# A row softmax on one core: six head loads of 16 rows per partition become three of 32

## The chip, the core and the metric

The kernel runs on one core of one Trainium2 chip. The time is device microseconds of one execution, the median of several. A core has the compute engines TensorE (PE, not used here), VectorE (DVE), ScalarE (ACT) and GpSimd (POOL); SyncE (SP) computes nothing and only issues transfers here. The transfers are carried out by the core's 16 DMA engines. On-chip memory has 128 partitions.

## The reference

The input is `x`, 16 x 1024 x 512 in float32: 16384 rows of 512 numbers, 33.55 MB. The output has the same shape. Each row is replaced by its softmax:

```python
x_max = np.max(x, axis=-1, keepdims=True)
exp_x = np.exp(x - x_max)
return (exp_x / np.sum(exp_x, axis=-1, keepdims=True)).astype(np.float32)
```

## The kernel before

The 16384 rows are spread over 128 partitions, 128 rows to each. "Row" below means one of these 128 rows per partition; row 5 is thus 128 rows of `x`, one in each partition, and takes 2 KiB of a partition.

**Groups.** Compute works on 16 groups of 8 rows. For each group there are four steps. DVE takes the negated row maxima (`rowmax`, line 164, an M in the order below). ACT runs eight activations, one per row, that write exp(x - max) over x and accumulate the row sums (line 195). DVE takes the reciprocals of the eight sums (line 170), and then either POOL (P in the order) or DVE (V) multiplies the group by them in place (line 172). The string `VECTOR` at line 44 is the order of DVE's instructions, written out by hand: `M5` is the maxima of group 5, `P4` the reciprocals of group 4 with the multiply on POOL, `V12` the reciprocals of group 12 with the multiply on DVE. DVE executes them in this order, and a step that has to wait holds up all that follow it there.

**Transfers.** All loads and stores are issued by SP on a single queue, in the order of the list `ORDER` (line 22): eight loads L and eight stores S, each of 16 rows, that is 32 KiB in each partition and 4 MiB in all. The first `AHEAD` entries (6) are loads issued at once at the start (line 126); the first of them is moved ahead of the program's opening barrier (`AT_HEAD`, line 49). Of the others, a store (line 152) waits on SP for the multiplies of the groups that it holds (`scaled`), and a load waits for the store whose place it takes (`stored`). SP waits in order: what stands behind a waiting entry of `ORDER` is not issued.

**The buffer.** `held` has room for 96 rows (`RING`). Loads (96,112) and (112,128) go to the places of rows 0 to 31 and so wait for stores (0,16) and (16,32). The numbers in brackets are the first row and the row after the last.

**Where rows lie in DRAM.** `in_dram` (line 87) takes the entry of `BLOCKS` that holds the rows and gives each partition a contiguous stretch of it: with a block of 16 rows, partition p has rows 16p to 16p + 15 of the block's 2048, so 32 KiB in one piece, and the next partition's piece follows at once. Loads and stores use the same mapping, so the output is independent of it.

**Semaphores.** Each load has its own semaphore (`loaded`), which the first `rowmax` that meets its rows waits for; `maxed`, `expd`, `to_pool` and `to_vector` pass groups from engine to engine.

Of the kernel before, what the change touches and what calls it, by code (L numbers as in the profile page):

```python
# [1 line left out]

# [4 lines left out]

F32 = mybir.dt.float32
EXP = mybir.ActivationFunctionType.Exp
AX = mybir.AxisListType.X  # L10

GROUP = 8
GROUPS = 16
RING = 12 * GROUP

BLOCKS = [(0, 16), (16, 32), (32, 48), (48, 64), (64, 80), (80, 96), (96, 112), (112, 128)]
ORDER = [
    ("L", (0, 16)),
    ("L", (16, 32)),
    ("L", (32, 48)),
    ("L", (48, 64)),
    ("L", (64, 80)),
    ("L", (80, 96)),
    ("S", (0, 16)),
    ("S", (16, 32)),  # L30
    ("S", (32, 48)),
    ("L", (96, 112)),
    ("L", (112, 128)),
    ("S", (48, 64)),
    ("S", (64, 80)),
    ("S", (80, 96)),
    ("S", (96, 112)),
    ("S", (112, 128)),
]
AHEAD = 6  # L40

VECTOR = """
    M0 M1 P0 M2 P1 M3 P2 M4 P3 M5 P4 M6 P5 M7 P6 M8 P7 M9 P8 M10 P9 M11
    P10 M12 P11 M13 V12 M14 V13 M15 V14 V15
"""

AT_HEAD = {mybir.EngineType.SP: 1}

def loads_at_the_head(nc):

    main, body = nc.main_func.blocks[0], nc.main_func.blocks[1]
    for engine, count in AT_HEAD.items():
        loads = [
            i
            for i in body.instructions
            if i.engine == engine and type(i).__name__ == "InstDMACopy"  # L60
        ][:count]
        barrier = next(
            n
            for n, i in enumerate(main.instructions)
            if i.engine == engine and type(i).__name__ == "InstDrain"
        )
        for load in loads:
            body.instructions.remove(load)
        main.instructions[barrier:barrier] = loads


@with_exitstack
def kernel(
    ctx: ExitStack,
    tc: tile.TileContext,
    x: bass.AP,
    out: bass.AP,
):
    nc = tc.nc
    nc.at_finalize(loads_at_the_head)  # L80
    P = nc.NUM_PARTITIONS

    d = x.shape[-1]
    x_rows, out_rows = x.flatten_outer_dims(), out.flatten_outer_dims()
    assert x_rows.shape[0] == GROUPS * GROUP * P

    def in_dram(rows, a, b):

        first, last = next(k for k in BLOCKS if k[0] <= a and b <= k[1])
        block = rows[first * P : last * P].rearrange("(p r) d -> p r d", p=P)  # L90
        return block[:, a - first : b - first, :]

    held = nc.alloc_sbuf_tensor("held", [P, RING, d], F32).ap()
    shift = nc.alloc_sbuf_tensor("shift", [P, GROUPS * GROUP], F32).ap()
    sums = nc.alloc_sbuf_tensor("sums", [P, GROUPS * GROUP], F32).ap()
    recip = nc.alloc_sbuf_tensor("recip", [P, GROUPS * GROUP], F32).ap()

    loads = [k for what, k in ORDER if what == "L"]
    stores = [k for what, k in ORDER if what == "S"]
    loaded = {k: nc.alloc_semaphore(f"loaded{k[0]}") for k in loads}  # L100
    scaled = [nc.alloc_semaphore(f"scaled{g}") for g in range(GROUPS)]
    stored = {k: nc.alloc_semaphore(f"stored{k[0]}") for k in stores}
    maxed = nc.alloc_semaphore("maxed")
    expd = nc.alloc_semaphore("expd")
    to_pool = nc.alloc_semaphore("to_pool")
    to_vector = nc.alloc_semaphore("to_vector")

    def take(engine, semaphore, n):

        engine.wait_ge(semaphore, n).then_inc(semaphore, -n)  # L110

    def rows(a, b):
        assert a // RING == (b - 1) // RING
        return held[:, a % RING : (b - 1) % RING + 1, :]

    def meets(k, a, b):
        return k[0] < b and a < k[1]

    def group(g):
        return g * GROUP, (g + 1) * GROUP  # L120

    def stats(t, g):
        return t[:, g * GROUP : (g + 1) * GROUP]

    def load(k):
        copy = nc.sync.dma_start(out=rows(*k), in_=in_dram(x_rows, *k))
        copy.then_inc(loaded[k], 16)
        return copy

    with tc.manual_schedule():
        for _, k in ORDER[:AHEAD]:
            tc.no_tile_sem_insts.add(load(k).ins.name)
    tc.close()
    tc.compile()  # L137

    taken, done = set(), set()
    for what, k in ORDER[AHEAD:]:  # L140
        if what == "L":
            for s in stores:
                if meets(s, k[0] - RING, k[1] - RING) and s not in taken:
                    take(nc.sync, stored[s], 16)
                    taken.add(s)
            load(k)
        else:
            for g in range(GROUPS):
                if meets(k, *group(g)) and g not in done:
                    take(nc.sync, scaled[g], 1)  # L150
                    done.add(g)
            nc.sync.dma_start(out=in_dram(out_rows, *k), in_=rows(*k)).then_inc(
                stored[k], 16
            )


    seen = set()

    def rowmax(g):
        for k in loads:  # L160
            if meets(k, *group(g)) and k not in seen:
                take(nc.vector, loaded[k], 16)
                seen.add(k)
        nc.vector.reduce_max(  # L164
            out=stats(shift, g), in_=rows(*group(g)), axis=AX, negate=True
        ).then_inc(maxed, 1)

    def scale(g, engine, ready):
        take(nc.vector, expd, 1)
        nc.vector.reciprocal(out=stats(recip, g), in_=stats(sums, g)).then_inc(ready, 1)  # L170
        take(engine, ready, 1)
        engine.tensor_mul(  # L172
            out=rows(*group(g)),
            in0=rows(*group(g)),
            in1=stats(recip, g).unsqueeze(2).to_broadcast([P, GROUP, d]),
        ).then_inc(scaled[g], 1)

    for step in VECTOR.split():
        what, g = step[0], int(step[1:])
        if what == "M":  # L180
            rowmax(g)
        elif what == "V":
            scale(g, nc.vector, to_vector)
        else:
            scale(g, nc.gpsimd, to_pool)


    nc.scalar.preload_act_table(EXP)  # L188

    with nc.scalar.Fori(0, GROUPS) as i:  # L190
        take(nc.scalar, maxed, 1)
        for r in range(GROUP):
            row = held[:, bass.ds(i % (RING // GROUP) * GROUP + r, 1), :]
            at = bass.ds(i * GROUP + r, 1)
            act = nc.scalar.activation(  # L195
                out=row,
                in_=row,
                func=EXP,
                bias=shift[:, at],
                scale=1.0,  # L200
                accum_out=sums[:, at],
            )
        act.then_inc(expd, 1)


    for k in stores:
        if k not in taken:
            take(nc.sync, stored[k], 16)


# [1 line left out]
_INS = ['x']  # L212
_OUTS = [((16, 1024, 512), 'float32')]


# [23 lines left out]
```

## Time and profile before

| | |
|---|---|
| median of 3 runs | 160.15 us (160.12 to 160.21) |
| the profiled execution | 160.14 us, with a span of 158.8 us |
| DVE busy | 90.6 us (57%) |
| ACT busy | 92.0 us (58%) |
| POOL busy | 84.0 us (53%) |
| DMA queue's packets | 98.9% of 16 engines' span |
| bytes moved | 33.55 MB read, 33.55 MB written, 423 GB/s |

The span runs from the first recorded instruction to the last event; the profiled execution's own time is 1.34 us longer. A figure such as x16 counts instructions. In the timelines a row gives its start in the span, the time to its end, the engine, the line of the kernel, the operation and the tiles, and in square brackets the idle time before it with what ended it; "held<-in_x_dram" is a load into `held`, "out_dram<-held" a store. A row of DMA issues gives the KB of each and the median time from issue to landing, the latter being when the completion has been seen. A row with x11 merges eleven instructions that follow each other. In a view by windows the columns are the stretch, its length, the busy time of DVE, ACT and POOL with their counts, the granted TensorE clock, the share of the DMA engines' time, and GB/s; a packet is booked in the stretch in which it starts, so shares can pass 1.

### The profile page before, as it was taken

What the parts mean: (1) busy time and instruction counts of PE and PEld (TensorE: products, weight loads), DVE (VectorE), ACT (ScalarE), POOL (GpSimd) and SP (SyncE); (2) the same over time, 40 slices, a digit from 0 to 9 for tenths busy, and PEclk for the clock granted to TensorE, in tenths of its full rate; (3) what the DMA queues carried; (4) which work ended last, traced back from release to release, by engine and by line L of the source; (5) the groups of instructions that cost most, each with busy time, mean ns of one, the idle gap of its engine ahead of it and who ended that gap; (6) DMA issues with size and microseconds to landing.
All of it is one profiled execution on the core that took longest, in us unless ns stands there. A gap on an engine that the chain in (4) does not pass through costs nothing. (4 is left out here: it accounts for less than half of the span.)

```text
span 158.8 us, 747 instructions
## 1 busy us (share of the span) xinstructions
DVE 90.6 (57%) x36; ACT 92.0 (58%) x257; POOL 84.0 (53%) x16
## 2 busy tenths in 40 slices
DVE  0008959777977977887700000795999998640000
ACT  0300699999999999999993000059934929200000
POOL 0000009999999999999999999259200000000000
DMA  7999999999999998999999999999999999999996
GB/s 264 470 454 396 413 487 421 396 454 470 396 396 487 437 396 380 413 396 454 470 396 421 462 437 396 446 479 396 421 446 454 396 437 473 413 404 454 446 413 264
DMA packets 2305, 67.12 MB, mean 423 GB/s; under 512 B 256, under 2 KB 256, under 8 KB 256
## 3 DMA queue, kind: packets, MB, share of 16 engines
q1 hardware_dynamic: 2304, 67.11, 98.9%
q14 instruction: 1, 0.01, 0.0%
HBM read 33.55 MB, written 33.55 MB: 423 GB/s over the span
## 5 line engine op out<-in xcount | busy, mean ns | idle before, releaser
L195 ACT ACTIVATE held<-held,shift x128 | 90.3, 712 | 40.0 <-ACTq L110 40.0
L172 POOL TENSOR_TENSOR held<-held,recip 128x4096 f32<-128x4096 f32 x12 | 83.8, 7015 | 28.0 <-POOLq L110 28.0
L164 DVE TENSOR_REDUCE shift<-held 128x8 f32<-128x4096 f32 x16 | 70.3, 4399 | 33.2 <-DVEq L110 33.2
L195 ACT ACTIVATION_READ_ACCUMULATOR held<-held,shift x128 | 24.6, 192 | 0.0
L172 DVE TENSOR_TENSOR held<-held,recip 128x4096 f32<-128x4096 f32 x4 | 18.3, 4570 | 0.6
L170 DVE RECIPROCAL recip<-sums 128x8 f32<-128x8 f32 x16 | 3.2, 201 | 16.5 <-DVEq L110 16.5
L188 ACT ACT_TABLE_LOAD x1 | 1.3, 1283 | 3.9 <-PEq L137 3.9
L223 POOL MEMSET const-float32-0.0<- 128x1 f32 x1 | 0.1, 98 | 0.2 <-issue 0.2
L223 POOL MEMSET const-uint8-127<- 128x1 uint8 x1 | 0.1, 102 | 0.0
L223 POOL MEMSET const-bfloat16-1.0<- 128x1 bf16 x1 | 0.1, 101 | 0.0
L223 POOL MEMSET const-float32-1.0<- 128x1 f32 x1 | 0.1, 98 | 0.0
## 6 DMA issues: line engine op xcount, KB each, us to landing
held<-in_x_dram SPq DMA_DIRECT2D x8, 4096.0 KB, 29.7
out_dram<-held SPq DMA_DIRECT2D x8, 4096.0 KB, 28.3
```

The costliest lines, as they stand in the source:

```text
L164: nc.vector.reduce_max(out=stats(shift, g), in_=rows(*group(g)), axis=AX, negate=True).then_inc(maxed, 1)
L170: nc.vector.reciprocal(out=stats(recip, g), in_=stats(sums, g)).then_inc(ready, 1)
L172: engine.tensor_mul(out=rows(*group(g)), in0=rows(*group(g)), in1=stats(recip, g).unsqueeze(2).to_broadcast([P, GROUP, d]),).then_inc(scal ...
L188: nc.scalar.preload_act_table(EXP)
L195: act = nc.scalar.activation(out=row, in_=row, func=EXP, bias=shift[:, at], scale=1.0, accum_out=sums[:, at],)
L223: nc = _bacc.Bacc("TRN2", target_bir_lowering=False, num_devices=1)
```

## The change

The six loads of rows 0 to 95 become three, of 32 rows each: 64 KiB in each partition, 8 MiB in all. `BLOCKS` follows them: the first 96 rows are laid out in DRAM in blocks of 32 rows, so that a load's 64 KiB of a partition are one contiguous piece. The stores of these rows stay at 16 rows, and each now takes half of every partition's 64 KiB. The last two loads, the last two stores and their blocks are as before. `AHEAD` is 3 in place of 6: the same rows are loaded at the start. In DVE's order, groups 12 and 13 are multiplied on POOL in place of DVE. With the blocks, row r of a partition holds another row of `x` than before, which changes no instruction.

```diff
-BLOCKS = [(0, 16), (16, 32), (32, 48), (48, 64), (64, 80), (80, 96), (96, 112), (112, 128)]
+BLOCKS = [(0, 32), (32, 64), (64, 96), (96, 112), (112, 128)]
 ORDER = [
-    ("L", (0, 16)),
-    ("L", (16, 32)),
-    ("L", (32, 48)),
-    ("L", (48, 64)),
-    ("L", (64, 80)),
-    ("L", (80, 96)),
+    ("L", (0, 32)),
+    ("L", (32, 64)),
+    ("L", (64, 96)),
     ("S", (0, 16)),
     ("S", (16, 32)),
     ("S", (32, 48)),
     ("L", (96, 112)),
     ("L", (112, 128)),
     ("S", (48, 64)),
     ("S", (64, 80)),
     ("S", (80, 96)),
     ("S", (96, 112)),
     ("S", (112, 128)),
 ]
-AHEAD = 6
+AHEAD = 3

 VECTOR = """
     M0 M1 P0 M2 P1 M3 P2 M4 P3 M5 P4 M6 P5 M7 P6 M8 P7 M9 P8 M10 P9 M11
-    P10 M12 P11 M13 V12 M14 V13 M15 V14 V15
+    P10 M12 P11 M13 P12 M14 P13 M15 V14 V15
 """
```

## The prediction

> **What bounds the kernel now.** I read the page's slices and queue table first, then the windows by stage, then the queue's own issues with their times to landing, last the engines' timelines. The first view says which resource is never idle:
>
> ```profile
> span 158.8 us, 747 instructions
> DVE 90.6 (57%) x36; ACT 92.0 (58%) x257; POOL 84.0 (53%) x16
> DMA  7999999999999998999999999999999999999996
> GB/s 264 470 454 396 413 487 421 396 454 470 396 396 487 437 396 380 413 396 454 470 396 421 462 437 396 446 479 396 421 446 454 396 437 473 413 404 454 446 413 264
> DMA packets 2305, 67.12 MB, mean 423 GB/s; under 512 B 256, under 2 KB 256, under 8 KB 256
> q1 hardware_dynamic: 2304, 67.11, 98.9%
> ```
>
> Three compute engines are each under 60% busy; the 16 DMA engines are full from the second slice to the last but one. 2304 packets are 16 transfers of 128 large packets (one partition's 32 KiB each) and of 16 small ones (the 256 "under 512 B"). The chain of waits shows only 3% of the span, because it does not follow the DMA queue; it is of no use here. Next, the rate by stage (columns: stretch, its length, DVE, ACT and POOL busy, clock, DMA share, GB/s):
>
> ```profile
> 42.00:52.00 10.00, 7.76 (x5) 10.00 (x29) 10.00 (x3) 1.00 0.99 429
> 52.00:57.00 5.00, 3.85 (x3) 5.00 (x15) 5.00 (x1) 1.00 0.97 419
> 57.00:62.00 5.00, 4.41 (x2) 5.00 (x15) 5.00 (x2) 1.00 0.98 347
> 62.00:72.00 10.00, 8.36 (x4) 10.00 (x29) 10.00 (x2) 1.00 1.04 449
> ```
>
> Bytes are booked when a packet starts, so 419 to 449 is one steady rate. 347 GB/s at 57 to 62 us, with the DMA engines as busy as ever, is a real dip: packets take longer there. It lies where the loads end and the first store begins. The issues put numbers on it (median us from issue to landing; the six loads in issue order):
>
> ```profile
> 1.17 0.42 SPq L126 DMA_DIRECT2D held<-in_x_dram  x1
> held<-in_x_dram SPq DMA_DIRECT2D x1, 4096.0 KB, 30.4
> ...
> 1.65 0.47 SPq L126 DMA_DIRECT2D held<-in_x_dram  x1
> held<-in_x_dram SPq DMA_DIRECT2D x1, 4096.0 KB, 39.7
> ...
> 65.44 0.33 SPq L152 DMA_DIRECT2D out_dram<-held  x1
> out_dram<-held SPq DMA_DIRECT2D x1, 4096.0 KB, 25.4
> ...
> 140.91 0.33 SPq L152 DMA_DIRECT2D out_dram<-held  x1
> out_dram<-held SPq DMA_DIRECT2D x1, 4096.0 KB, 17.9
> ```
>
> Issue plus time to landing gives the landings. Loads: the first at 12.2, the second at 0.79 + 21.0 = 21.8 (the median of the first two is 16.6, midway from 12.2), the third at 1.17 + 30.4 = 31.6, the fourth at 41.4, the fifth at 2.16 + 48.9 = 51.05 and the sixth near 61.5 by the medians of neighbouring pairs. Stores (0,16), (16,32), (32,48): 71.1, 80.9, 90.8. Loads (96,112), (112,128): 100.3, 110.1. The last five stores: 119.9, 129.6, 139.4, 149.1, 158.8. So 4 MiB lands every 9.7 us, in order of issue, and the span ends with the sixteenth. Two places cost more: the first landing takes 12.2 us, 2.5 us over the pitch, and the sixth load is 10.5 us behind the fifth, a stall of 0.8 us. The turn from load (112,128) to store (48,64) at 110 us shows none.
>
> Last, how far compute is ahead of this queue:
>
> ```profile
> 12.33 8.75 DVE L164 TENSOR_REDUCE shift<-held 128x8 f32<-128x4096 f32 x2 [12.33 <-DVEq L110]
> 23.46 76.76 POOL L172 TENSOR_TENSOR held<-held,recip 128x4096 f32<-128x4096 f32 x11 [23.02 <-POOLq L110]
> 105.16 7.01 POOL L172 TENSOR_TENSOR held<-held,recip 128x4096 f32<-128x4096 f32 x1 [4.94 <-POOLq L110]
> ```
>
> Store (32,48) is issued at 65.4 and its turn comes at 80.9, when the store before it lands. A transfer issued before its turn costs the end nothing.
>
> **The change, part by part.**
>
> *Fewer, longer packets.* Six loads of 128 x 32 KiB become three of 128 x 64 KiB. Bytes are the same. Each DMA engine gets 24 large packets in place of 48, and 3 fewer small ones. No packet of 64 KiB is in the trace, so I bound it. Fixed part of a packet: in a 0.4 us window the one 8 KiB instruction packet has 4.8% of 16 engines, 0.307 us; from 22 to 52 us, 400 large packets have 101.2% of 30 us x 16, 1.214 us each. Four times 0.307 is 1.228, so (1.228 - 1.214) / 3 = 5 ns is fixed per packet (1 to 9 ns with the rounding of 4.8%). 24 packets fewer save 0.12 us (0.02 to 0.2). The small packets: 8 x 1.214 = 9.71 us is already the pitch, so three of them are at most 0.03 us. The other end: the pitch between like neighbours varies from 9.69 to 9.78 us; should the long packets sit at its upper end, six times 0.05 is a loss of 0.3. I take -0.15, because the steady rows are the nearest, and keep -0.25 and +0.3.
>
> The Trainium skill, page "DMA: Bandwidth & Descriptors", section "Bandwidth", gives one transfer about 2.0 us fixed plus bytes at 436 GB/s, and advises large transfers. By that, three transfers fewer would save 6 us, an estimate from the page. The trace disagrees for a queue that is never empty: 9.7 us per 4 MiB is 432 GB/s with the fixed part in it.
>
> *Three SP issues less.* Six take 3.13 us at the start, three some 1.6. They lie beside the first load, and the first one stays at 0. Nothing.
>
> *The first data come later.* Row maxima 0 wait for 8 MiB: the second load's landing now, 21.8 in place of 12.2. DVE, ACT and POOL all start 9.6 us later. What it meets, with POOL's 76.76 / 11 = 6.98 us per group: P0 starts at 33.1, so store (0,16) is issued at 37.5 + 9.6 = 47.1 (turn at 61.5), (16,32) at 61.1 (turn 71.1), (32,48) at 75.0 (turn 80.9). The last has least room, 5.9 us. SP then issues load (96,112), which stands behind it on SP, at about 75.4 where it was 71.28; its turn is at 90.8. Load (112,128) still waits for store (16,32), landed at 80.9. Store (48,64) follows P7 at 89 (turn 110.1), (64,80) P9 at 103 (119.9), (80,96) P11 at 117 (129.6). Row maxima 4 and 8, which now wait for loads landing near 41.2 and 61.3, come at 44 and 67. ACT's 12 groups end near 94.4, still before load (96,112) lands. All hidden; cover gone means one us per us beyond these margins.
>
> *Groups 12 and 13 go from DVE to POOL.* DVE loses two of its 4.43 to 5.00 us multiplies, POOL gains two of 7.01. POOL: P11 ends at 117, P12 at 124, P13 at 131; store (96,112) is issued at 131 (125.6 before; turn 139.4, 8 us of room). On DVE, M14 no longer stands behind V12 (started 111.45), nor M15 behind V13, so V15 ends near 133 in place of 140.8; store (112,128) follows at 133 (turn 149.1). Neither bounds. Nothing.
>
> *The stores keep 32 KiB per partition*, but in the first 96 rows their pieces, and the loads' rows, now lie 64 KiB apart in DRAM instead of 32. No row shows another pitch; see the rivals. I take nothing. The 0.8 us stall I keep: the first store still follows an unbroken run of loads.
>
> **Sum.** The profiled execution took 160.14 (span 158.8 and 1.34 around it), against a median of 160.15. 158.8 - 0.15 + 1.34 = 160.0 us. Range of this case alone: 159.85 to 160.45.
>
> **The rivals.**
>
> *The stall goes* (faster): it comes once, after 48 large packets in a row, and not at 110 us after 16. If the long run of queued packets causes it, 24 of them may not. Against it: what is special may simply be the first store, which stays. 160.0 - 0.8 = 159.2.
>
> *The stall grows* (slower): only packets in flight at the turn at 57 to 62 us are stretched, 0.8 us on 32 KiB ones. If it scales with the packet, the last 64 KiB packets lose 1.6: 160.8. It is slower by my bound from a stall of 1.3 us on.
>
> *The pitch in DRAM* (slower): 12 of the 16 transfers, 116 us, now run with rows 64 KiB apart. One per cent of rate lost there is 1.2 us: 161.2; it decides from 0.4%. Nothing in the trace shows sensitivity: loads and stores, in all regions, keep 9.7 us. The Trainium skill, same page, section "Latency and other measured facts", has copies slowing at large power-of-two row pitches, from 207 GB/s each way at 512 KiB to 164 at 2 MiB; by that 64 KiB is still harmless. No run here shows it.
>
> *The queue runs dry* (slower): it needs store (32,48) after 80.9, that is compute 15.5 us late instead of 9.6. Were POOL a whole group (6.98 us) further behind, 9.6 + 7.0 - 15.5 = 1.1 us: 161.1.
>
> *A fixed cost per transfer* (faster): if the first landing's 2.5 us over the pitch were paid by every load, three fewer give 160.14 - 7.5 = 152.6. The 9.7 us pitch speaks against it. The skill's formula above would give 154.1.
>
> *The row is cut in two again* by the queue, and packets stay 32 KiB: 160.14.
>
> **How the numbers follow.** Plain small gain 0.67 (160.0); cut rows 0.05 (160.14); stall gone 0.11; stall grown 0.09; pitch 0.05; dry queue 0.02; fixed cost 0.01. A change below 0.2% (0.32 us) is about what a measurement of this kernel cannot tell from none. Faster 0.11 + 0.01 = 0.12, same 0.72, slower 0.16. The range takes in both stall cases with 0.1 us to spare, 159.1 to 160.9; pitch, dry queue and fixed cost, 0.08, stay outside.
>
> **What would show it.** Right: 1872 packets on the queue (13 x 16 small, 384 of 64 KiB, 1280 of 32 KiB; 2256 if the rows are cut), DMA full from slice 2 to 39, landings of loads near 21.8, 41.2 and 61.4, then every 9.7 us; POOL starting at 33; SP never issuing a store after its turn. Wrong: a landing pitch other than 9.7 in the first 96 rows, a different dip near 57 to 62 us, or a slice of DMA below 9 in the middle.

## The result: 0.2% slower, where 0.1% faster was forecast

The changed kernel takes 160.49 us (median of 13 runs, 160.36 to 161.26) against 160.12 for the kernel before in the same comparison: a ratio of 1.0022, with a 95% interval of 1.0012 to 1.0032. The forecast was 160.0, with 159.1 to 160.9 as its range and 0.16 for "slower". The time lies in the range; the sign is wrong. It lies 0.04 us above the range that I gave this case alone, 159.85 to 160.45. The wide range holds it only because it had room for a longer stall, and I had given that another reason.

The page of the changed kernel, the lines that answer to those shown of before:

```profile
span 159.2 us, 741 instructions
DVE 88.0 (55%) x34; ACT 91.8 (58%) x257; POOL 102.1 (64%) x18
DMA  7996996997989989999999999999999999999994
DMA packets 1873, 67.12 MB, mean 422 GB/s; under 512 B 208, under 2 KB 208, under 8 KB 208
q1 hardware_dynamic: 1872, 67.11, 98.6%
```

1872 packets: a row of 64 KiB in one partition does move whole. The queue still never runs empty. By the trace's packet records a 64 KiB packet takes 2.418 us and a 32 KiB packet 1.213. (A digit below 9 in the first slices of DMA comes from long packets being booked where they start.)

The same stretches as before in the view by windows, of the changed kernel:

```profile
52.00:57.00 5.00, 3.84 (x3) 5.00 (x15) 5.00 (x2) 1.00 0.97 419
57.00:62.00 5.00, 3.85 (x3) 5.00 (x15) 5.00 (x2) 1.00 1.02 354
62.00:72.00 10.00, 7.99 (x3) 10.00 (x31) 10.00 (x2) 1.00 1.03 446
72.00:82.00 10.00, 8.61 (x4) 10.00 (x30) 10.00 (x3) 1.00 0.99 426
82.00:92.00 10.00, 5.06 (x4) 10.00 (x29) 10.00 (x3) 1.00 0.97 419
```

and the last stretch of the kernel before:

```profile
82.00:92.00 10.00, 0.00 (x0) 2.91 (x9) 10.00 (x2) 1.00 0.97 419
```

The dip at the turn from loads to stores is still there. What differs is beside store (32,48), from 82 to 92 us: ACT is busy for all of it where it was busy for 2.9 us, because compute runs 9.7 us later.

Where do the 0.35 us of the span come from? The issue of load (112,128), which SP makes when store (16,32) has landed, and its time to landing; first before, then after:

```profile
80.96 0.34 SPq L126 DMA_DIRECT2D held<-in_x_dram  x1
held<-in_x_dram SPq DMA_DIRECT2D x1, 4096.0 KB, 29.1
```

```profile
81.06 0.34 SPq L123 DMA_DIRECT2D held<-in_x_dram  x1
held<-in_x_dram SPq DMA_DIRECT2D x1, 4096.0 KB, 29.3
```

Up to 81 us 0.10 us are lost; by the landing at 110.06 and 110.36, 0.30. So 0.2 us go in between, while the transfers are the same as before.

A transfer has landed when the last of the 16 DMA engines is done with it, and each engine works through its own share of every transfer, 8 of the 128 large packets. The packet records do not name the engine; a packet is put down to the engine whose packet before it ended as this one started. The small packets that end each engine's share show the spread. After 158.2 us there are, before and then after, in 158.2:158.5 and 158.5:158.9:

```profile
DMA packets 2, 0.00 MB, mean 0 GB/s; under 512 B 2, under 2 KB 2, under 8 KB 2
DMA packets 0, 0.00 MB, mean 0 GB/s; under 512 B 0, under 2 KB 0, under 8 KB 0
```

```profile
DMA packets 1, 0.00 MB, mean 0 GB/s; under 512 B 1, under 2 KB 1, under 8 KB 1
DMA packets 1, 0.00 MB, mean 0 GB/s; under 512 B 1, under 2 KB 1, under 8 KB 1
```

The last engine ends at 158.31 us before; after, one ends at 158.34 and the last at 158.65. By the packet records, from the first packet's start to the first engine's end is 156.42 us before and 156.38 after, and to the mean of the 16 ends 156.80 in both: the engines as a whole are no slower. From the first engine's end to the last one's is 0.87 before and 1.25 after. In both kernels this last engine is one whose packets, from 66 us on, often take 14 to 50 ns (once 130) more than 1.213, several one after the other, while the others' hardly ever do. (In the kernel before, two engines start a packet in the same nanosecond at 135.25 us. I follow the one whose packets go on being long; if they are the other way round, the slowed engine ends at 158.24 and not last.)

### The profile page after: what moved, and what is told of

It reads as the page before. It is cut to its first block, busy times and chain, and to the rows that moved or that the text cites. A ratio compares the mean times of both kernels' runs of the same rounds, so it can differ in the third digit from the quotient of the medians.

```text
span 159.2 us, 741 instructions
## 1 busy us (share of the span) xinstructions
DVE 88.0 (55%) x34; ACT 91.8 (58%) x257; POOL 102.1 (64%) x18
## 3 DMA queue, kind: packets, MB, share of 16 engines
q1 hardware_dynamic: 1872, 67.11, 98.6%
## 5 line engine op out<-in xcount | busy, mean ns | idle before, releaser
L169 POOL TENSOR_TENSOR held<-held,recip 128x4096 f32<-128x4096 f32 x14 | 101.9, 7315 | 32.7 <-POOLq L107 32.7
L192 ACT ACTIVATION_READ_ACCUMULATOR held<-held,shift x128 | 25.1, 196 | 0.0
L169 DVE TENSOR_TENSOR held<-held,recip 128x4096 f32<-128x4096 f32 x2 | 15.7, 7857 | 0.3
```

Source lines behind the costliest of these rows:

```text
L169: engine.tensor_mul(out=rows(*group(g)), in0=rows(*group(g)), in1=stats(recip, g).unsqueeze(2).to_broadcast([P, GROUP, d]),).then_inc(scal ...
L192: act = nc.scalar.activation(out=row, in_=row, func=EXP, bias=shift[:, at], scale=1.0, accum_out=sums[:, at],)
```

## The experiments

Two numbers are read from each trace's packet records. *Long packets beside stores* is the time that packets take above their plain 1.213 or 2.418 us (0.611 for the 16 KiB packets of early8_fine), summed over all engines, from 66 to 81 us (stores (0,16) and (16,32)) and from 81 to 91 us (store (32,48)). *The turn* is the same sum from 56 to 61 us, divided by 16: what an engine loses there. Times are medians; the ratio is to the kernel before on the same chip. The ratio is not the plain quotient of the two medians, and differs from it by up to 0.0009, or 0.15 us.

| kernel | us (before) | ratio, 95% interval | long packets, 66-81 / 81-91, ns | turn, us |
|---|---|---|---|---|
| before | 160.12 | | 296 / 47 | 0.88 |
| changed | 160.49 (160.12) | 1.0022 (1.0012 to 1.0032) | 279 / 277 | 1.01 |
| swap_only | 160.14 (160.20) | 0.9994 (0.9981 to 1.0008) | 302 / 51 | 0.81 |
| loads_only | 160.48 (160.20) | 1.0012 (0.9998 to 1.0027) | 293 / 293 | 1.06 |
| late_only | 160.34 (160.20) | 1.0010 (0.9995 to 1.0024) | 280 / 248 | 0.71 |
| layout_only | 160.39 (160.20) | 1.0009 (0.9995 to 1.0023) | 295 / 84 | 1.03 |
| early_big | 160.57 (160.20) | 1.0021 (1.0012 to 1.0030) | 312 / 208 | 0.96 |
| early8 | 160.04 (160.20) | 0.9992 (0.9983 to 1.0000) | 282 / 102 | 0.61 |
| act_only | 160.00, one run | | 181 / 42 | 0.63 |
| no_act | 166.48, one run | | 0 / 0 | 0.74 |
| copy16 | 159.80 (160.20) | 0.9966 (0.9954 to 0.9979) | 0 / 61 | 0.65 |
| copy32 | 160.09 (160.20) | 0.9991 (0.9982 to 1.0001) | 0 / 0 | 1.07 |
| loads32_old | 160.31 (160.20) | 1.0005 (0.9995 to 1.0016) | 284 / 310 | 0.85 |
| turn_early | 160.32 (160.20) | 1.0005 (0.9996 to 1.0014) | see below | see below |
| copy_load64 | 160.04 (160.21) | 0.9989 (0.9980 to 0.9998) | 0 / 0 | 1.04 |
| copy_store64 | 159.77 (160.21) | 0.9977 (0.9968 to 0.9985) | 0 / 0 | 0.85 |
| act_no_sum | 159.95, one run | | 40 / 74 | 0.72 |
| early8_fine | 160.16 (160.25) | 0.9995 (0.9981 to 1.0008) | 295 / 116 | 0.67 |
| early8_again | 160.12 (160.25) | 0.9992 (0.9983 to 1.0002) | 296 / 175 | 0.52 |

The 61 of copy16 lies at the end of its stretch, where store (32,48) gives way to a load. Other kernels have long packets there too while ACT rests: copy_load64 one of 219 ns at 92.5 us, act_only one of 87 at 92.2, early8 80 in all from 88 to 91. So the second column is not ACT's alone. In the changed kernel 132 of its 277 ns are one packet at 89.1 us. From 81 to 88 us, clear of that place, the sums are 21 before and 136 in the changed kernel, 116 in late_only, 126 in loads_only and loads32_old, 98 in early_big, 19 in layout_only and early8.

**The parts of the change, one at a time.** Four theories: late compute, the swap to POOL, the layout in DRAM, the long packets.

```diff
 swap_only, to the kernel before:
-    P10 M12 P11 M13 V12 M14 V13 M15 V14 V15
+    P10 M12 P11 M13 P12 M14 P13 M15 V14 V15
```

> The kernel before with groups 12 and 13 multiplied on POOL (P12, P13 for V12, V13) and nothing else. Layout and packet theories, and late compute: no change, within 0.1 us of the kernel before. Theory of the swap (POOL and DVE hold each other up at the end, V15 took 10.6 us in the changed kernel): 0.3 us slower, most of the 0.37 us that the changed kernel lost.

```diff
 loads_only, to the changed kernel:
-    P10 M12 P11 M13 P12 M14 P13 M15 V14 V15
+    P10 M12 P11 M13 V12 M14 V13 M15 V14 V15
```

> The changed kernel with V12, V13 kept: three loads of 32 rows, compute 9.6 us late, no swap. Theory of the swap: 0.05 to 0.15 us faster than the kernel before. The three others (late compute, layout, long packets): 0.25 to 0.4 us slower, as the changed kernel.

```diff
 late_only, to the kernel before, in rowmax:
-            if meets(k, *group(g)) and k not in seen:
+            if meets(k, *(group(g) if g else (0, 32))) and k not in seen:
```

> The kernel before, all transfers as they were, but the first row maxima wait for load (16,32) too, so compute runs 9.6 us later. Theory of late compute (more work of ACT and DVE lies beside the stores, one DMA engine of the 16 is slowed by it, and the slowest ends the kernel): 0.2 to 0.4 us slower, and the skew between the first and the last DMA engine's end grows from 0.87 us toward 1.2. Layout and packets: within 0.1 us, skew unchanged.

```diff
 layout_only, to the kernel before:
-BLOCKS = [(0, 16), (16, 32), (32, 48), (48, 64), (64, 80), (80, 96), (96, 112), (112, 128)]
+BLOCKS = [(0, 32), (32, 64), (64, 96), (96, 112), (112, 128)]
```

> The kernel before with the DRAM blocks of the changed kernel (pieces of 32 KiB, 64 KiB apart) but still six loads of 16 rows. Theory of the layout: 0.25 to 0.4 us slower. Late compute, long packets and swap: within 0.1 us.

The swap costs nothing: the loss is there without it (160.48, though the interval just reaches no change) and not with it alone (160.14). Neither late compute (+0.14) nor layout (+0.19) is the whole, and each one's interval by itself still contains no change; but their traces differ in two distinct places. Late compute alone raises the long packets beside store (32,48) from 47 to 248 ns, and the spread of the engines at the end from 0.87 to 1.17 us, toward the changed kernel's 1.25; the layout does not make packets long in this place (84, and 19 up to 88 us), though its spread is 1.00. The layout alone raises the turn to 1.03 us with packets of 32 KiB; late compute does not (0.71).

**Early compute with long loads.**

```diff
 early_big, to the changed kernel:
-    ("L", (0, 32)),
+    ("L", (0, 16)),
+    ("L", (16, 32)),
-AHEAD = 3
+AHEAD = 4
```

> The changed kernel with its first load cut in two again, (0,16) and (16,32), both in the block of 32 rows: compute starts as early as in the kernel before, two of the three long loads stay, and so does the layout. Theory of late compute: the part of the loss that comes from 79 to 91 us (0.2 us on one DMA engine) is gone, 160.1 to 160.3. Theory of layout and packets alone: as slow as the changed kernel, 160.4 to 160.6.

It gained nothing, 160.57. The edit did not keep compute early. DVE in this kernel, at row maxima 4:

```profile
41.24 4.42 DVE L162 TENSOR_REDUCE shift<-held 128x8 f32<-128x4096 f32 x1 [6.89 <-DVEq L108]
```

They wait 6.9 us for the long load (32,64), so ACT runs beside store (32,48) again (208 ns), and the layout is still there. The run does not tell the theories apart.

**Which engine's work makes the packets long.**

```diff
 act_only, to the kernel before:
-        nc.vector.reduce_max(out=stats(shift, g), in_=rows(*group(g)), axis=AX, negate=True).then_inc(maxed, 1)
+        nc.vector.memset(stats(shift, g), 0.0).then_inc(maxed, 1)
...
-        nc.vector.reciprocal(out=stats(recip, g), in_=stats(sums, g)).then_inc(ready, 1)
-        take(engine, ready, 1)
-        engine.tensor_mul(...).then_inc(scaled[g], 1)
+        nc.vector.reciprocal(out=stats(recip, g), in_=stats(sums, g)).then_inc(scaled[g], 1)
```

> The kernel before without its row maxima (DVE writes zeros of 128x8 instead) and without its multiplies: ACT's exponentials with their sums are what is left beside the transfers. If ACT's work is what slows one DMA engine beside stores, the skew between the first and the last DMA engine still grows from about 0.5 us after the loads to 0.75 or more at the end. If DVE or POOL does it, it stays within 0.15 us of its value after the loads (but for the one instruction fetch).

```diff
 no_act, to the kernel before (the loop of activations is left out):
+        if g >= 6:
+            nc.vector.reduce_max(out=stats(sums, g), in_=rows(*group(g)), axis=AX, negate=True)
         nc.vector.reduce_max(
             out=stats(shift, g), in_=rows(*group(g)), axis=AX, negate=True
-        ).then_inc(maxed, 1)
+        ).then_inc(maxeds[g], 1)
...
-        take(nc.vector, expd, 1)
-        nc.vector.reciprocal(out=stats(recip, g), in_=stats(sums, g)).then_inc(ready, 1)
+        take(nc.vector, maxeds[g], 1)
+        nc.vector.reciprocal(out=stats(recip, g), in_=stats(shift, g)).then_inc(ready, 1)
```

> The kernel before without its exponentials (reciprocals of the maxima instead of the sums); from group 6 on DVE takes each maximum twice, so that DVE and POOL are busy beside the first three stores. If ACT's work slows the engine, no engine is slowed and the skew stays within 0.15 us of its value after the loads (but for the one instruction fetch). If DVE or POOL does it, the skew grows by 0.2 us or more over those stores.

The windows of the kernel without ACT (here the columns are DVE and POOL):

```profile
62.00:72.00 10.00, 10.00 (x5) 10.00 (x3) 1.00 1.00 433
72.00:82.00 10.00, 10.00 (x4) 10.00 (x2) 1.00 0.99 429
82.00:92.00 10.00, 10.00 (x4) 8.86 (x2) 1.00 0.99 426
```

DVE and POOL never rest, and no packet is long: 0 / 0. (Its total time means nothing: the doubled maxima of the last groups issue the last store too late.) ACT alone, in the other kernel (DVE, ACT, POOL):

```profile
62.00:72.00 10.00, 0.46 (x4) 10.00 (x29) 0.00 (x0) 1.00 1.01 436
72.00:82.00 10.00, 0.20 (x1) 8.71 (x26) 0.00 (x0) 1.00 0.98 423
82.00:92.00 10.00, 0.00 (x0) 0.00 (x0) 0.00 (x0) 1.00 0.99 429
```

181 ns of long packets while ACT runs, on one engine, and 42 once it rests. So ACT's work beside stores slows the one engine, and DVE and POOL without ACT do not. ACT alone does not give all of the 296 ns of the kernel before: whether DVE and POOL add to ACT's effect is open. A little is there without ACT as well: in the kernel before, packets that take 13 to 23 ns more still come at 138.9 to 141.3 us, after ACT's last instruction. The spread at the end, which I had expected to tell, did not: in act_only it grew to 0.92 and in no_act, at the turn from load (112,128) to a store, to 1.06. That turn too can stretch packets, by 0.01 us an engine in the kernel before and 0.13 in no_act; why it differs is not known. Is it the read-out of the sums?

```diff
 act_no_sum, to act_only:
-                accum_out=sums[:, at],
...
-        nc.vector.reciprocal(out=stats(recip, g), in_=stats(sums, g)).then_inc(scaled[g], 1)
+        nc.vector.memset(stats(recip, g), 0.0).then_inc(scaled[g], 1)
```

> As the kernel with ACT's exponentials alone, but without the sums that each activation reads out. If ACT's instructions as such slow the DMA engine beside stores: 0.05 to 0.2 us of long packets again from 65 to 80 us. If it is the read-out of the sums: none there.

40 ns, against 181, just under the 0.05 that I had put as the least. But without the sums ACT is done with its first twelve groups at 72.0 us in place of 80.7. Beside the later stores both kernels have long stretches of ACT; here are act_only and act_no_sum (DVE, ACT, POOL), then no_act (DVE, POOL):

```profile
109.00:124.00 15.00, 0.69 (x5) 14.43 (x42) 0.00 (x0) 1.00 1.01 435
```

```profile
109.00:124.00 15.00, 0.29 (x5) 11.71 (x20) 0.00 (x0) 1.00 1.02 441
```

```profile
109.00:124.00 15.00, 14.85 (x7) 7.01 (x1) 1.00 1.00 431
```

The long packets in this stretch sum to 247 and 202 ns, which is 17 ns per microsecond of ACT's work in both, with 42 instructions or with 20. In no_act they sum to 7, apart from one packet stretched by an instruction fetch. So the read-out of the sums is not needed, nor does the effect go by the number of ACT's instructions. What of an ACT instruction does it stays open; short, frequent instructions on another engine were not tried.

**Transfers without compute.**

```diff
 copy16, to the kernel before, and copy32, to the changed kernel (all compute is left out):
-            for g in range(GROUPS):
-                if meets(k, *group(g)) and g not in done:
-                    take(nc.sync, scaled[g], 1)
-                    done.add(g)
+            for m in loads:
+                if meets(m, *k) and m not in done:
+                    take(nc.sync, loaded[m], 16)
+                    done.add(m)
```

> The transfers of the kernel before with no compute at all: a store waits only for its load. Theory of ACT beside stores: no engine is slowed by compute, so the skew between the first and last DMA engine stays within 0.15 us of its value after the loads, and the time is 0.2 to 0.4 us below the kernel before. If the skew grows as before, ACT is not its cause.

> The transfers of the changed kernel with no compute at all. Two theories of what is left besides late compute. Packets only: 0.1 us faster than the copy with 16-row loads. Layout (the stall at the turn from loads to stores is larger when rows lie 64 KiB apart; packets that took more than 1.02 of their plain time at 55 to 62 us sum to 15 to 17 us over the 16 engines in four kernels with the new blocks, 10 to 14 us in six with the old): 0.1 to 0.3 us slower than the copy with 16-row loads, with the difference at the turn.

Without compute no engine is slowed beside the stores, and the transfers of the kernel before take 159.80. The spread did not stay as I had expected: in copy16 it goes from 0.73 after the loads to 0.97, all of it at the turn at 110 us, so the spread at the end is no sign of compute by itself. The changed transfers still lose 0.29 us by the medians, with intervals that do not meet, so late compute is not the whole. Which side of the layout does it:

```diff
 copy_load64, to copy16:
+WIDE = [(0, 32), (32, 64), (64, 96), (96, 112), (112, 128)]
...
-        copy = nc.sync.dma_start(out=rows(*k), in_=in_dram(x_rows, *k))
+        copy = nc.sync.dma_start(out=rows(*k), in_=in_dram(x_rows, *k, WIDE))
 copy_store64, to copy16:
-            nc.sync.dma_start(out=in_dram(out_rows, *k), in_=rows(*k)).then_inc(
+            nc.sync.dma_start(out=in_dram(out_rows, *k, WIDE), in_=rows(*k)).then_inc(
```

> No compute, 16-row transfers; the loads take their rows from blocks of 32 (rows 64 KiB apart in DRAM), the stores from blocks of 16 as before, so rows change places. If the loads' layout makes the larger stall at the turn: 16 to 17 us of long packets there, 160.0 to 160.1 us. If the stores' layout does: 10 to 12 us and the time of the copy with 16-row blocks, 159.8.

> No compute, 16-row transfers; the stores go to blocks of 32 rows (64 KiB apart), the loads come from blocks of 16 as before, so rows change places. If the stores' layout makes the larger stall: 16 to 17 us of long packets at the turn and 160.0 to 160.1 us. If the loads' layout does: 10 to 12 us and 159.8.

It is the loads', by the turn (1.04 us against 0.85) and the landing below; the intervals of the two times still overlap a little. SP issues load (96,112) when the first store has landed; the rows of copy16, copy32, copy_load64 and copy_store64 in this order:

```profile
71.25 10.03 SPq L126 DMA_DIRECT2D held<-in_x_dram  x2
```

```profile
71.57 10.03 SPq L123 DMA_DIRECT2D held<-in_x_dram  x2
```

```profile
71.52 10.03 SPq L127 DMA_DIRECT2D held<-in_x_dram  x2
```

```profile
71.34 10.02 SPq L127 DMA_DIRECT2D held<-in_x_dram  x2
```

With the loads' rows 64 KiB apart the first store lands at 71.52 and 71.57, with 32 KiB at 71.25 and 71.34; in the first pair one kernel has packets of 64 KiB and one of 32. Over all profiles the turn costs 0.96 to 1.07 us in the six with loads from blocks of 32 rows, and 0.52 to 0.88 in the twelve others that have the turn in this place. The kernel before, at 0.88, is the highest of these, so its own profile understates the difference.

**Both causes, one taken back.**

```diff
 loads32_old, to the changed kernel (BLOCKS as before; a load takes two of them):
+        if b - a == 32:
+            two = rows[a * P : b * P].rearrange("(k p r) d -> p k (r d)", k=2, p=P)
+            return two
```

> The changed kernel with the DRAM blocks of the kernel before: each load of 32 rows takes two blocks of 16 rows, so its packets are 32 KiB again and rows lie 32 KiB apart; compute is late and groups 12 and 13 are on POOL as in the changed kernel. Layout theory: the turn's stall goes back by 0.2 to 0.3 us and the time is 160.2 to 160.35, as with late compute alone. If late compute were the whole of it: 160.45 to 160.6, as the changed kernel or slower by the lost packet gain.

160.31, with the turn back at 0.85 and the long packets of late compute (310) still there: as the layout theory has it. The interval again contains no change.

**Is there something better?**

```diff
 turn_early, to the kernel before:
-    ("L", (80, 96)),
     ("S", (0, 16)),
+    ("L", (80, 96)),
-AHEAD = 6
+AHEAD = 5
```

> The kernel before with store (0,16) issued ahead of load (80,96): the first turn from loads to stores comes at 51 us, after five loads, and a second and third turn follow. If the 0.8 us stall belongs to the first store after the loads, it moves to 51 us and the time is as before, 160.1 to 160.3; if it belongs to a queue of six loads, it goes and the time is 159.3 to 159.5; if every turn costs, 160.5 or more.

The stall moves with the first store: 0.72 us an engine from 46 to 51 us, and a second, smaller one of 0.13 from 66 to 71. Nothing is gained.

```diff
 early8, and again early8_again, to the kernel before:
-    ("L", (0, 16)),
+    ("L", (0, 8)),
+    ("L", (8, 16)),
-AHEAD = 6
+AHEAD = 7
 early8_fine, to early8 (BLOCKS likewise):
-    ("L", (80, 96)),
+    ("L", (80, 88)),
+    ("L", (88, 96)),
...
-    ("S", (80, 96)),
+    ("S", (80, 88)),
+    ("S", (88, 96)),
-AHEAD = 7
+AHEAD = 8
```

> The kernel before with its first load cut in (0,8) and (8,16): compute starts near 7.4 us in place of 12.3. Theory of late compute: ACT's first twelve groups end near 80 us, before store (32,48) runs, so the slow engine loses a little less there: 0 to 0.1 us faster than before. If only the number of transfers counted: 0.02 us slower. A loss above 0.1 us would speak against the theory.

> The kernel with its first load cut in (0,8) and (8,16), and besides the last head load and its store cut in two, each in a DRAM block of 8 rows, so that rows lie 16 KiB apart just ahead of the turn. If the stall follows the spacing downwards too, it loses 0.1 to 0.3 us and the time is 159.8 to 160.0; if not, the two more transfers and their 16 KiB packets cost 0.05 to 0.2 us: 160.1 to 160.25.

> The kernel before with its first load cut in (0,8) and (8,16), again: 160.0 to 160.1 us against 160.2 if the earlier compute is a gain; equal to the kernel before if the first comparison was chance.

early8 is the fastest full kernel, 0.13 to 0.16 us below the kernel before in both comparisons, though each interval reaches 1. My reason for it is not borne out: ACT's first twelve groups ended at 83.3 us, not near 80 (84.9 before), and the long packets from 81 to 91 us did not fall (102 and 175 against 47; 19 and 28 against 21 up to 88 us). The finer last load brought nothing more; the turn does not follow the spacing downwards (0.67).

## Why the prediction was wrong

- *What bounds it*: right. The queue stayed full, store (32,48) was issued at 75.2 (75.0 forecast) for its turn at 81, and no wait of SP became the bound.
- *Fewer, longer packets*, -0.15: right in the packet records. The second long load ends 19.32 us behind the first on the first engine; two loads of 16 rows took 19.36. Three times 0.044 is 0.13. In the times it does not show: copy32, with long packets, takes 160.09, and copy_load64, with 16-row ones, 160.04, each known to some 0.15 us. The Trainium skill, page "DMA: Bandwidth & Descriptors", has the formula that I set against this term, 2.0 us fixed for each transfer, not in "Bandwidth" but in the section "Anatomy of one DMA — SWDGE (gpsimd) path", for transfers that GpSimd issues. All of these are issued by SP, in a queue that is never empty.
- *"I take nothing. The 0.8 us stall I keep"*: the first step that failed. The turn lost some 0.24 us more by the medians (159.80 to 160.04 without compute and with the same packets; 0.37 by the ratios) because the loads' rows lie 64 KiB apart. I had this cause as the rival of the pitch, but as a rate lost over 116 us, and this place as the rival of the growing stall, but with the packets' length as its reason. It is the pitch, of the loads, paid once at the turn. The steady rate did not change: stores 64 KiB apart still took 9.68 us each. The Trainium skill, page "DMA: Bandwidth & Descriptors", section "Latency and other measured facts", has copies at 207 GB/s each way with a pitch of 512 KiB, where 214 is full; it has no smaller pitch and says nothing of the turn.
- *The first data come later, "All hidden"*: the second step that failed. The margins of each store were right, and I priced only a missed turn. Work that is later also lies beside other transfers: beside store (32,48) the slowest engine lost 0.2 us more (248 to 310 ns against 47), of which some 0.1 us, up to 88 us, is clear of the turn to the load behind it. In time that was 0.14 us in late_only and 0.11 in loads32_old, neither clear of the noise: that late compute costs time rests on the traces more than on these two.
- *Groups 12 and 13 on POOL*, nothing: right in the sum (swap_only 0.9994), wrong in its detail. I had V15 end at 133; DVE's last multiply took 10.61 us beside POOL's in place of 4.43, and POOL ended at 135.0, not 131:

```profile
128.71 10.61 DVE L169 TENSOR_TENSOR held<-held,recip 128x4096 f32<-128x4096 f32 x1
```

Store (96,112) was issued at 135.1 for its turn at 139.4; half of the room that I had counted was gone.

Packets, turn and late compute give -0.13 + 0.24 + 0.14 = 0.25 us; the transfers as a whole without compute and late compute give 0.29 + 0.14 = 0.43. Measured were 0.37, with 0.19 to 0.51 as the interval, and the parts are no surer than that. In the two profiles themselves the gain of the packets (0.13 us) and the longer turn (1.01 against 0.88) cancel, since this profile of the kernel before has a long turn. There the whole difference is in the spread, and 0.17 us of it is where the slow engine happened to lie among the 16 after the first store (0.14 us behind the first engine before, 0.31 after); no run explains that.

## What to carry to other kernels

When a DMA queue is never empty, the end is set by the slowest of its 16 engines, so look at the spread of their ends, not at the mean share. Work that is "hidden" still has neighbours: ask not only whether it is in time for its turn, but which transfers it will now lie beside. A larger load can also change how rows lie in DRAM, as it did here; test the layout apart from the size, as one line of the block table did here.

## What the runs showed of the hardware that was not expected

- ACT's work beside stores slows one DMA engine of 16 by 14 to 50 ns on many of its 1.21 us packets, 0.18 us from 66 to 81 us with ACT alone (act_only) and 0.3 with all engines at work; DVE and POOL at full load without ACT slow none (no_act, 0).
- The first turn from loads to stores costs each engine 0.5 to 0.9 us with loads' rows 32 KiB apart, and 0.96 to 1.07 with 64 KiB; it goes where the first store goes. Why the spacing of loads matters there is open.
- One instruction fetch of 8 KiB stretches one engine's packet by 0.35 to 0.43 us (0.36 in the changed kernel at 133.8 us, 0.43 in early8_again at 126.4). In the changed kernel that engine ended second to last, at 158.34 us.
